# A hybrid decoder layer: cached-row attention started with each head's own column tiles, its products tied to the weight units, cached rows loaded some steps ahead

## The chip, the cores and the metric

The kernel runs on one core of a Trainium2 chip, as one launch. The metric is the device time of that launch in microseconds (us). TensorE (PE) multiplies matrices, VectorE (DVE), ScalarE (ACT) and GpSimd (POOL) do the elementwise work, and SyncE (SP) issues DMAs. Each engine works through its own instructions in order.

## The reference

One layer of a decoder for 512 prompt rows and 64 sample rows (8 sequences of 8 new tokens), model width 2048, all in float32:

```python
proj = rms_norm(x) @ w_in                       # 2048 -> 7168 columns, split among three mixers
ya = gate_b * causal_dwconv3(gate_c * xa)       # mixer A, 512 columns
for g, (window, dilation) in enumerate(((128, 1), (512, 4), (2048, 16))):
    # mixer B, 4 heads of 128: keys at distances 0, d, 2d, ..., window;
    # the sample rows read them from a cache of `window` K and V rows per sequence and head
    s_j = q . k[pos - j * d] / sqrt(128) - slope * j * d
    o_g, lse_g = softmax_j(s) @ v, logsumexp_j(s)
yb = sum_g softmax_g(lse) * o_g
yc = scale * ((trailing_mean_w(u) - u) @ w_pool)  # mixer C, w = 2, 4, 8, 16
x = x + concat(ya, yb, yc) @ w_out
x = x + (silu(dwconv3(h2 @ w_gate)) * (h2 @ w_up)) @ w_down     # h2 = rms_norm(x)
```

The outputs are the normed x and the new caches and states.

## The kernel before

Activations stand transposed: 128 features on the partitions, 576 tokens (512 prompt, 64 sample) along the free axis, as two halves of 288. A float32 product is made of three passes over rounded parts: weights are split into `wh` (ACT, L141) and `wl = wr - wh` (DVE, L142), activations likewise, and `mm3` (L150) adds wh·xh, wh·xl and wl·xh.

**Column tiles.** `project` (L159) makes one tile of 128 output columns from 16 blocks of w_in in two weight units of 8 blocks: one unit is a 512 KB load, one `wh`, one `wl` and 48 matmuls of 288 columns. Weight tiles have three buffers each, so `wl` of the next units is made while PE works on one. The accumulator `acc` has two buffers; a DVE instruction takes a finished tile out of PSUM, for attention into a tile `t` (L589, L592). Two of the tiles are made with the first norm, 54 more follow: 9 for each of 4 heads (q, k, v for three groups), 8 for pooling (4 each after the second and third head), 12 for the gated convolution. The out projection and the feed-forward part follow.

**What hangs on a head's tiles.** After each v tile, `natural` (L330) transposes that group's k and v on PE (L337, L346, L347) through the small PSUM tiles `ps` (two buffers), ACT copies them out, and DMAs store them into the outputs and into a DRAM scratch `kvd`. After the ninth tile `att_prompt` (L359) does the prompt attention on PE, DVE and ACT.

**Sample attention** is written as generators: `sample_scores` (L423) has 27 steps per head, one for 128x1024 products of the query broadcast `qb` with cached K rows `ek` (POOL, L433) and their row sums (DVE, L434); `sample_values` (L459) has 4 steps for the softmax, 13 for cached V rows `ev` (8 steps of eight DVE multiply-adds each for the far group, L516 and L519; 5 steps of `collect`, small matmuls, L497) and one for the new rows. `ek` has two buffers, `ev` three. After each column tile `step` (L562) lets the generators advance by the rates `RATE_MAIN`, `RATE_POOL`, `RATE_TAIL` (steps per tile, scores and values); a head's scores are queued after its ninth tile, its values after its scores. The scheduler then places the instructions of each engine; a load (`dma_paced`) is written in the step that uses it. All DMAs are issued by SP.

**Pooling tiles** (L622): `sp_nat` loads the old state, PE transposes it (L634), DVE copies it into `ec` (L636), POOL and DVE add shifted copies (L644), DVE forms `t` (L650, L652), ACT and DVE split it (L174, L175) into `ek` tiles, and `pool_map` (L666) multiplies two of those with a small weight, 24 matmuls on both `acc` buffers. `sp_nat` shares its two buffers (tag `ob`) with the output tiles of `att_prompt`.

Of the kernel before, what the change touches and what calls it, by code (L numbers as in the profile page):

```python
# [16 lines left out]
P = 128  # L17
# [23 lines left out]
RATE_MAIN = (2.5, 2.5)  # L41
RATE_POOL = (1.5, 1.0)
RATE_TAIL = (4.5, 5.0)
# [37 lines left out]
def decoder_step(ctx: ExitStack, tc, I, O):  # L81
    nc = tc.nc
    dma = nc.sync.dma_start
    PS = bass.MemoryType.PSUM
# [64 lines left out]

    def mm3(acc, wh, wl, xt, first, last):  # L150
        for h in range(2):
            xh = xt[:, 0, h * HALF:(h + 1) * HALF]
            xl = xt[:, 1, h * HALF:(h + 1) * HALF]
            o = acc[:, h, :HALF]
            nc.tensor.matmul(o, wh, xh, start=first, stop=False)  # L155
# [3 lines left out]
    def project(w, c0, xs, order, ahead=()):  # L159
        acc = acc_tile()  # L160
        n = len(order)
        for u in range(0, n, 8):
            ks = order[u:u + 8]
            k0 = min(ks)
            hi, lo = ahead[u // 8] if u // 8 < len(ahead) else wunit(w, k0, len(ks), c0)
            for j, k in enumerate(ks):
# [163 lines left out]
    def natural(g, h, k, v):  # L330

        for kv, t in ((0, k), (1, v)):
            blocks = [3] if g == 0 and kv == 0 else [0, 1, 2, 3]
            pt = ps_tile()
            for a in blocks:
                src = t[:, a * P:(a + 1) * P] if g == 0 else class_view(t, a)
                nc.tensor.transpose(pt[:, a * P:(a + 1) * P], src, ident)  # L337
            b0 = blocks[0]
            n = at.tile([P, 4, P], F32, tag=("kn", "vn")[kv], bufs=(1, 3)[kv], name=nm("nat"))
            nc.scalar.copy(n[:, b0:, :], pt[:, b0 * P:].rearrange("p (a d) -> p a d", d=P))  # L340
            if g == 0:
                dma(kvp[0][:, kv, h, :], n[:, 3, :])
            else:
                dma(kvp[g][:, kv, h, :].rearrange("(i r) d -> i r d", r=4), n)
        pt = ps_tile()
        nc.tensor.transpose(pt[:64, 0:P], smp(k), ident)  # L346
        nc.tensor.transpose(pt[:64, P:2 * P], smp(v), ident)  # L347
        ns = at.tile([64, 2 * P], F32, tag="ns", bufs=2, name=nm("ns"))
        nc.scalar.copy(ns, pt[:64, :2 * P])
        win = DILS[g][0]  # L350
        for kv in range(2):
            dma(kvs[g][:, win - 8:win, kv, h, :], ns[:, kv * P:(kv + 1) * P])
        dma(kvd[h].rearrange("(b i) v g d -> b i v g d", i=16)[:, 0:8, :, g, :], ns)
        return n
# [50 lines left out]
    def sample_queries(q):  # L405

        pt = ps_tile()
        for g in range(3):
            nc.tensor.transpose(pt[:64, g * P:(g + 1) * P], smp(q[g]), ident)
        qn = at.tile([64, 3 * P], F32, tag="qn", bufs=1, name=nm("qn"))  # L410
        nc.scalar.copy(qn, pt[:64, :3 * P])
        qd = dp.tile([3, 64, P], F32, name=nm("qd"))
        dma(qd.rearrange("g r d -> r g d"), qn.rearrange("r (g d) -> r g d", g=3))
        return qd
# [8 lines left out]
    def sample_scores(h, qd, st):  # L423

        for g in (2, 1, 0):
            qb = at.tile([P, 1024], F32, tag="qb", bufs=2, name=nm("qb"))
            dma_paced(qb, qd[g].rearrange("(b t) d -> b (t d)", b=NB).unsqueeze(1).to_broadcast([NB, 16, 1024]))
            qv = qb.rearrange("p (a j d) -> p j a d", a=2, d=P)
            rows = cache_rows(g, 0, h)

            def one(sl_, keys, prod):
                pv_ = prod.rearrange("p (a j d) -> p j a d", a=2, d=P)
                nc.gpsimd.tensor_mul(pv_, qv, keys)  # L433
                nc.vector.tensor_reduce(st[:, sl_, :].rearrange("p (j a) -> p j a", a=2), pv_, axis=AX.X, op=ALU.add)  # L434

            for u in range((1, 4, 8)[g]):
                kt = eslot_raw("ek", 1024)
                dma_paced(kt.rearrange("p (s d) -> p s d", d=P), rows[:, u])
                if g == 2:
                    one(19 + u, kt.rearrange("p (a j d) -> p j a d", j=4, d=P), kt)  # L440
                    yield
                    continue
                for e in range((8, 2)[g]):
                    nk = (1, 4)[g]
                    kb = kt[:, e * nk * P:(e + 1) * nk * P].rearrange("p (j d) -> p j d", d=P).unsqueeze(2)
                    one((e, 8 + 2 * u + e)[g], kb.to_broadcast([P, 4, 2, P]), prod_tile())
                    yield
            kn = at.tile([P, P], F32, tag="kvn", bufs=2, name=nm("kn"))
            dma_paced(kn, kvd[h][:, 0, g, :])
            one(16 + g, kn.unsqueeze(1).unsqueeze(1).to_broadcast([P, 4, 2, P]), prod_tile())  # L450
            yield
# [7 lines left out]
    def sample_values(h, st, yb):  # L459

        sx = st.rearrange("p s t -> p (s t)")
# [43 lines left out]
        for g in (2, 1, 0):  # L505
            rows = cache_rows(g, 1, h)
            for u in range((1, 4, 8)[g]):
                vt = eslot_raw("ev", 1024)
                v = vt.rearrange("p (s d) -> p s d", d=P)
                dma_paced(v, rows[:, u])  # L510
                if g == 2:
                    for t in range(8):
                        pos = 2 * (t % 4) + t // 4
                        w = st[:, 19 + u, pos:pos + 1]
                        if u:
                            nc.vector.scalar_tensor_tensor(av[:, t, :], v[:, t, :], w, av[:, t, :],  # L516
                                                           op0=ALU.mult, op1=ALU.add)
                        else:
                            nc.vector.tensor_scalar(av[:, t, :], v[:, t, :], w, None, op0=ALU.mult)  # L519
                elif g == 1:  # L520
                    collect([(j, ((8 + 2 * u + e) * 8 + 2 * j) * 8, v[:, 4 * e + j, :])
                             for e in range(2) for j in range(4)])
                else:
                    collect([(j, (i * 8 + 2 * j) * 8, v[:, i, :]) for i in range(8) for j in range(4)])
                yield
        vt = at.tile([P, 3, P], F32, tag="vnn", bufs=1, name=nm("vnn"))
        dma_paced(vt, kvd[h][:, 1])
        collect([(j, ((16 + g) * 8 + 2 * j) * 8, vt[:, g, :]) for g in range(3) for j in range(4)])
        yield
# [10 lines left out]
        if h == 3:  # L540
            late[7] = yb
        else:
            dma(y_d[4 + h], yb)


    scores, values = [], []
    clock = [0, 0.0, 0.0]
    hooks = {}
# [13 lines left out]
    def step(rs, rv):  # L562
        for fn in hooks.pop(clock[0], []):
            fn()
        clock[1] = pump(scores, clock[1] + rs)
        clock[2] = pump(values, clock[2] + rv)
        clock[0] += 1

    def in_proj(c0):
        return project(w_in, c0, xk, allk)  # L570
# [7 lines left out]
    def head_tiles(h):  # L578
        q, k, vn = [], [], []
        for g in range(3):  # L580
            for s in range(3):
                c0 = ATT0 + g * 1536 + s * 512 + h * P
                acc = None if c0 in first else in_proj(c0)
                t = t576()
                if c0 in first:
                    nc.vector.tensor_mul(t, first[c0], rstd1)
                    (q, k)[s].append(t)
                elif s == 0:
                    nc.vector.scalar_tensor_tensor(halves(t), acc, SC, halves(rstd1), op0=ALU.mult, op1=ALU.mult)  # L589
                    q.append(t)  # L590
                else:
                    nc.vector.tensor_mul(halves(t), acc, halves(rstd1))  # L592
                    if s == 1:
                        k.append(t)
                    else:
                        vn.append(natural(g, h, k[g], t))
                if (g, s) == (2, 2):
                    yb = at.tile([P, TOK], F32, tag="yb", bufs=2, name=nm("yb"))
                    att_prompt(h, q, k, vn, yb)
                    qd = sample_queries(q)  # L600
                    st = at.tile([P, 27, 8], F32, tag="st", bufs=2, name=nm("st"))
                    scores.append((sample_scores(h, qd, st),
                                   lambda: values.append((sample_values(h, st, yb), lambda: None))))
                yield
# [8 lines left out]
    def state_rows(src, n, outs):  # L613
# [5 lines left out]
        for dst, a, b in outs:  # L619
            dma(dst, so[a:b, :])  # L620
# [45 lines left out]
    def pool_map(gi, dsl):  # L666
        hi, lo = wload(pw[gi].rearrange("(k p) c -> p k c", p=P), 512, (("p (k c) -> p k c",), dict(k=2)))
        for m in range(2):
# [7 lines left out]
            dma(y_d[8 + j], z)  # L676
# [64 lines left out]
    def take(gen, n):  # L741
        for _ in range(n):
            if next(gen, gen) is gen:
# [690 lines left out]
```

## Time and profile before

| | us |
|---|---|
| median of three runs (2701.39 to 2705.43) | 2703.88 |
| the profiled execution | 2703.15 |
| its span | 2701.3 |
| PE busy in the span | 2563.4 (95%) |
| PE busy from 60 to 1050 us | 924.71 of 990 |
| DVE, ACT, POOL busy in the span | 1916.6, 959.8, 640.7 |

Matmuls are pipelined, so one that takes 300 ns follows the one before it after some 130 ns, and a busy PE is one that never ran dry. The column tiles and the attention lie in the stretch from 60 to 1050 us, with the first of the out projection.

### The profile page before, as it was taken

To read this page: it belongs to the slowest core of one execution; us is meant where nothing else is said; L and a number is where in the kernel's file an instruction comes from. 1 tells how busy PE (TensorE), PEld (TensorE's weight loads), DVE (VectorE), ACT (ScalarE), POOL (GpSimd) and SP (SyncE) were. 2 spreads that over 40 slices of the span, in tenths; PEclk is the share of its full clock that TensorE was granted. 3 is DMA by queue.
4 is the path that set the end of the run, shared out by engine and by line. 5 is a ranking of instruction groups with operands and counts; after the bars stand their busy time and mean duration, and the time that the engine had idled before them with its cause. 6 is when DMAs were issued, how large, how long until landed. Compare 5 with 4: busy or idle time off the path is not lost.

```text
span 2701.3 us, 48714 instructions
## 1 busy us (share of the span) xinstructions
PE 2563.4 (95%) x19855; PEld 2511.3 (93%) x19855; DVE 1916.6 (71%) x2664; ACT 959.8 (36%) x1393; POOL 640.7 (24%) x490
## 2 busy tenths in 40 slices
PE   8998998999898999999999999999999798989997
PEld 8988998998888899999999999999999797989897
DVE  5236468458567744488787888888887988898885
ACT  6121221221121233354444444444444434343335
POOL 0017126225436200012222221212121112121114
PEclk9998998999999999999999999999999899999999
DMA  8335258259547695645555555555555745545534
GB/s 259 112 99 158 79 165 233 76 151 242 141 124 201 189 285 187 195 140 169 163 169 156 175 156 168 164 166 170 168 164 169 261 139 162 158 145 150 166 91 144
DMA packets 605106, 446.31 MB, mean 165 GB/s; under 512 B 22423, under 2 KB 568898, under 8 KB 598482
## 3 DMA queue, kind: packets, MB, share of 16 engines
q1 hardware_dynamic: 604882, 443.19, 55.4%
q8 instruction: 156, 2.56, 0.4%
q14 instruction: 68, 0.56, 0.1%
HBM read 400.53 MB, written 129.86 MB: 196 GB/s over the span
## 4 chain that ended last, share of the span: by engine, by line
PE 72%; DVE 10%; DMA 7%; issue 5%; POOL 4%; ACT 1%; SPq 1%; DVEq 0%; POOLq 0%; ACTq 0%
PE acc L839 27%; PE pt L839 7%; PE ps L839 7%; PE acc L155 7%; PE s L839 7%; PE acc L156 7%; PE acc L157 7%; DMA ek<-in_cache_kv_w_dram 3%; DVE av L516 2%; POOL eq L433 2%; POOL prod L433 2%; DVE wl L142 1%; DVE wl L828 1%; DVE st L434 1%; DVE xs L175 1%
## 5 line engine op out<-in xcount | busy, mean ns | idle before, releaser
L155 PE MATMUL acc<-xs,wh 128*128 128x288 f32 x2208 | 664.6, 302 | 5.7 <-DVE t L700 3.9
L156 PE MATMUL acc<-xs,wh 128*128 128x288 f32 x2208 | 661.6, 300 | 0.0
L157 PE MATMUL acc<-xs,wl 128*128 128x288 f32 x2208 | 659.7, 299 | 0.7 <-DVE wl L142 0.7
L827 ACT ACTIVATE wh<-wr 128x640 fp32r<-128x640 f32 (+1 forms) x396 | 343.4, 876 | 642.7 <-DVE wr L889 189.6
L828 DVE TENSOR_TENSOR wl<-wr,wh 128x640 fp32r<-128x640 f32 (+1 forms) x396 | 416.6, 1059 | 104.6 <-ACT wh L827 100.7
L155 PEld LDWEIGHTS acc<-xs,wh 128*128 128x128 f32 x2208 | 421.2, 191 | 13.2 <-issue 8.8
L839 PE MATMUL acc<-xs,wh 128*128 128x288 f32 x2048 | 419.2, 296 | 9.6 <-DVE wk L1289 5.0
L157 PEld LDWEIGHTS acc<-xs,wl 128*128 128x128 f32 x2208 | 423.4, 192 | 3.2 <-issue 1.8
L156 PEld LDWEIGHTS acc<-xs,wh 128*128 128x128 f32 x2208 | 422.1, 191 | 2.9 <-issue 2.5
L141 ACT ACTIVATE wh<-wr 128x1024 fp32r<-128x1024 f32 (+1 forms) x150 | 155.6, 1038 | 568.8 <-PE acc L156 513.9
L839 PEld LDWEIGHTS acc<-xs,wh 128*128 128x128 f32 x2048 | 330.3, 189 | 12.1 <-DVE wk L1289 6.4
L142 DVE TENSOR_TENSOR wl<-wr,wh 128x1024 fp32r<-128x1024 f32 (+1 forms) x150 | 218.4, 1456 | 130.7 <-ACT wh L141 127.6
L839 PE MATMUL acc<-xs,wl 128*128 128x288 f32 x1024 | 302.1, 295 | 0.3 <-DVE wl L828 0.3
L839 PE MATMUL acc<-x,wh 128*128 128x288 f32 x1196 | 246.0, 297 | 8.1 <-ACT wh L827 8.1
L901 POOL TENSOR_TENSOR wx<-wx,wr 128x1024 f32<-128x1024 f32 x43 | 116.6, 2711 | 454.9 <-DVE wl L828 369.2
L839 PEld LDWEIGHTS acc<-x,wh 128*128 128x128 f32 x1196 | 193.7, 190 | 8.9 <-ACT wh L827 8.8
L828 DVE TENSOR_TENSOR wl<-wx,wh 128x1024 fp32r<-128x1024 f32 x129 | 168.7, 1308 | 46.0 <-ACT wh L827 44.4
L839 PEld LDWEIGHTS acc<-xs,wl 128*128 128x128 f32 x1024 | 193.3, 189 | 0.7 <-DVE wl L828 0.7
L839 PE MATMUL acc<-x,wl 128*128 128x288 f32 x598 | 178.2, 298 | 6.0 <-DVE wl L828 6.0
L827 ACT ACTIVATE wh<-wx 128x1024 fp32r<-128x1024 f32 x129 | 136.8, 1062 | 100.4 <-PE ps L839 37.5
L433 POOL TENSOR_TENSOR ek<-qb,ek 128x1024 f32<-128x1024 f32 x32 | 78.7, 2465 | 270.6 <-DMA qb<-qd 176.4
L839 PE MATMUL s<-xs,wh 128*128 128x288 f32 x660 | 138.7, 299 | 3.3 <-ACT wh L827 3.3
(402 smaller groups left out, 4988.8 us busy)
## 6 DMA issues: line engine op xcount, KB each, us to landing
out_dram<-in_cache_kv_w_dram SPq DMA_DIRECT2D x320, 204.0 KB
wr<-in_w_in_dram SPq DMA_DIRECT2D x110, 512.0 KB
wr<-in_w_down_dram SPq DMA_DIRECT2D x128, 320.0 KB
ek<-in_cache_kv_w_dram SPq DMA_DIRECT2D x52, 512.0 KB
ev<-in_cache_kv_w_dram SPq DMA_DIRECT2D x52, 512.0 KB
wx<-in_w_gate_dram SPq DMA_DIRECT2D x43, 512.0 KB
wr<-in_w_gate_dram SPq DMA_DIRECT2D x43, 512.0 KB
wr<-in_w_up_dram SPq DMA_DIRECT2D x43, 512.0 KB
```

The source lines that it names most:

```text
L141: nc.scalar.activation(hi[:, :n], dst, AF.Copy)
L142: low.tensor_sub(lo[:, :n], dst, hi[:, :n].bitcast(F32))
L155: nc.tensor.matmul(o, wh, xh, start=first, stop=False)
L156: nc.tensor.matmul(o, wh, xl, start=False, stop=False)
L157: nc.tensor.matmul(o, wl, xh, start=False, stop=last)
L175: nc.vector.tensor_sub(dst[1], src, dst[0].bitcast(F32))
L433: nc.gpsimd.tensor_mul(pv_, qv, keys)
L516: nc.vector.scalar_tensor_tensor(av[:, t, :], v[:, t, :], w, av[:, t, :], op0=ALU.mult, op1=ALU.add)
L827: nc.scalar.activation(hi[:, :n], src, AF.Copy)
L828: nc.vector.tensor_sub(lo[:, :n], src, hi[:, :n].bitcast(F32))
L839: nc.tensor.matmul(o, a[:, ws], b, start=first and k == 0 and i == 0, stop=k == n - 1 and i == 2, skip_group_check=True)
L901: nc.gpsimd.tensor_sub(b21, b21, b11)
```

## The change

The sample attention of a head is queued before its first tile, and each of its steps starts when what it needs is there (`have`). A head's tiles come in the order q0, k0, q1, k1, q2, k2, v0, v1, v2. The generators advance after each weight unit (`tick`, called in `project`) by half a rate, and the rates are new. Each product on POOL, and the first of the eight DVE instructions of a far V step, wait for the first matmul of the unit written last (`with_unit`). `in_turn` writes the loads of up to three steps ahead of the step that runs, as far as its buffers go. Far and near V steps alternate. The transposes of a tile (`rows_of`) and the prompt attention (`prompt`) are posted to a later tick. 113 output DMAs are issued by ACT (`adma`), in place of 93 by SP.

```diff
-RATE_MAIN = (2.5, 2.5)
-RATE_POOL = (1.5, 1.0)
-RATE_TAIL = (4.5, 5.0)
+RATE_MAIN = (2.3, 1.9)
+RATE_POOL = (2.0, 1.8)
+RATE_TAIL = (3.0, 3.2)
...
+    adma = nc.scalar.dma_start
...
+    def with_unit(ins):
+        tc.add_manual_dep(ins.ins, unit[0], mybir.DependencyInfo(mybir.DependencyClass.Sync,
+                                                                 mybir.DependencyReason.DATA),
+                          reason="paced by the products")
...
                 mm3(acc, hi[:, ws], lo[:, ws], xs[k], u + j == 0, u + j == n - 1)
+            unit[0] = mark[0].ins.name
+            if tick:
+                tick()
...
+        adma(kvd[h].rearrange("(b i) v g d -> b i v g d", i=16)[:, 0:8, kv, g, :], ns)
+        adma(kvs[g][:, win - 8:win, kv, h, :], ns)
...
+    def in_turn(steps, have, room):
+        at_ = [0]
+        def loads(to):
+            while at_[0] < min(to, len(steps)):
+                need, ls, _, keep = steps[at_[0]]
+                if not all(x in have for x in need) or (ls and keep >= 0 and sum(held_.values()) >= room):
+                    return
+                for load in ls:
+                    load()
+                if ls and keep >= 0:
+                    held_[keep] = 1
+                at_[0] += 1
+        held_ = {}
+        for i in range(len(steps)):
+            keep = steps[i][3]
+            while at_[0] <= i:
+                loads(i + 1)
+                if at_[0] <= i:
+                    yield
+            loads(i + 3)
+            steps[i][2]()
...
-                nc.gpsimd.tensor_mul(pv_, qv, keys)
+                with_unit(nc.gpsimd.tensor_mul(pv_, c["q"], keys))
...
+        yield from in_turn(group(0) + group(1) + group(2), have, 2)
...
+                if t == 0:
+                    with_unit(i_)
...
+        for i, n_ in enumerate(near):
+            steps.insert(2 * i + 1, n_)
+        steps.append(([("v", g) for g in range(3)], [load_new], new_sum, -1))
+        yield from in_turn(steps, have, 3)
...
-    def step(rs, rv):
+    def tick():
         for fn in hooks.pop(clock[0], []):
             fn()
-        clock[1] = pump(scores, clock[1] + rs)
-        clock[2] = pump(values, clock[2] + rv)
+        clock[1] = pump(scores, clock[1] + rate[0][0] / 2)
+        clock[2] = pump(values, clock[2] + rate[0][1] / 2)
         clock[0] += 1
...
+        for g, s in ((0, 0), (0, 1), (1, 0), (1, 1), (2, 0), (2, 1), (0, 2), (1, 2), (2, 2)):
...
+            post(1, lambda g=g, s=s, t=t: rows_of(g, s, t))
+            if (g, s) == (2, 2):
+                post(1, prompt)
+            yield
```

**The transposes after a v tile, on PE.** Before, second head, second group: `acc_300` is that v tile, `t576_307` holds it, and `acc_318` is the next tile.

```order
L157 MATMUL acc_300_2396<-xs_99_596,wl_306_2454 128x288
L337 MATMUL ps_308_2507<-ident_72,t576_296_2386 128x128 x4
L155 MATMUL acc_318_2542<-xs_24_151,wh_320_2545 128x288
...
L156 MATMUL acc_318_2542<-xs_56_318,wh_320_2545 128x288
L337 MATMUL ps_310_2515<-ident_72,t576_307_2505 128x128 x4
L346 MATMUL ps_312_2523<-ident_72,t576_296_2386 64x128
L347 MATMUL ps_312_2523<-ident_72,t576_307_2505 64x128
L157 MATMUL acc_318_2542<-xs_56_318,wl_321_2546 128x288
```

The transposes of `t576_307` stand 32 matmuls after the end of its tile. In the change that tile is `acc_385`, its copy `t576_405`, and `acc_406` is the tile after it:

```order
L168 MATMUL acc_385_2773<-xs_99_596,wl_394_2840 128x288
...
L168 MATMUL acc_406_2926<-xs_99_596,wl_416_3001 128x288
L351 MATMUL ps_417_3052<-ident_72,t576_405_2924 128x128 x4
L360 MATMUL ps_419_3060<-ident_72,t576_405_2924 64x128
L166 MATMUL acc_429_3092<-xs_24_151,wh_431_3095 128x288
```

They moved behind all 96 matmuls of the next tile.

**The same copy out of PSUM, on DVE.** Before, `L434` rows are sums of POOL's products, and `L592` is the copy:

```order
L142 TENSOR_TENSOR wl_324_2600<-wr_322_2597,wh_323_2599 128x1024
L434 TENSOR_REDUCE st_236_1765<-eq_328_2658 128x8
L434 TENSOR_REDUCE st_236_1765<-prod_338_2774 128x8
L434 TENSOR_REDUCE st_236_1765<-eq_341_2781 128x8
L592 TENSOR_TENSOR t576_307_2505<-acc_300_2396,rstd1_82 128x576
L142 TENSOR_TENSOR wl_332_2665<-wr_330_2662,wh_331_2664 128x1024
```

In the change (`L693` is the copy, `L490` the sums, `L584` far V steps):

```order
L584 SCALAR_TENSOR_TENSOR av_401_2909<-ev_404_2914,st_122_766,av_401_2909 128x128 x3
L693 TENSOR_TENSOR t576_405_2924<-acc_385_2773,rstd1_82 128x576
L584 SCALAR_TENSOR_TENSOR av_401_2909<-ev_404_2914,st_122_766,av_401_2909 128x128 x4
L143 TENSOR_TENSOR wl_432_3096<-wr_430_3093,wh_431_3095 128x1024
L490 TENSOR_REDUCE st_359_2614<-prod_411_2983 128x8
L562 COPY os_400_2908<-ps_413_2988 128x128
L584 SCALAR_TENSOR_TENSOR av_401_2909<-ev_404_2914,st_122_766,av_401_2909 128x128
L143 TENSOR_TENSOR wl_438_3165<-wr_436_3162,wh_437_3164 128x1024
```

Three sums in a row ahead of the copy became parts of one far V step, and the sums stand one by one between the units.

**The first pool map after the prompt attention, on PE.** Before, `ek_421` and `ek_441` are the split inputs of the first two pooling tiles, and `L634` the state transposes of the second and the fourth:

```order
L634 MATMUL ps_426_3286<-ident_72,sp_nat_425_3284 128x120
...
L155 MATMUL acc_467_3577<-ek_421_3273,wh_465_3573 128x288
...
L634 MATMUL ps_476_3621<-ident_72,sp_nat_475_3619 128x120
L155 MATMUL acc_467_3577<-ek_441_3418,wh_465_3573 128x288
```

In the change (`L729` are the state transposes of the second and third pooling tile, `L711` stores the new state, `ek_520` is the second tile's split input):

```order
L729 MATMUL ps_497_3472<-ident_72,sp_nat_496_3470 128x120
...
L711 MATMUL ps_508_3599<-ident_72,sst_491_3457 120x128
...
L166 MATMUL acc_539_3784<-ek_494_3465,wh_537_3780 128x288
...
L729 MATMUL ps_523_3646<-ident_72,sp_nat_522_3644 128x120
...
L166 MATMUL acc_539_3784<-ek_520_3639,wh_537_3780 128x288
L166 MATMUL acc_541_3800<-ek_520_3639,wh_537_3780 128x288
```

From the second tile's state transpose to the map that needs that tile there were 126 matmuls of 288 columns; now there are 44, because the transpose moved behind the prompt attention, whose output tiles hold the buffers of `sp_nat`.

## Rows read from the trace of the kernel before

**Rows 1.** The page's 40 equal slices of the span, some 67.5 us each.

```profile
PE   8998998999898999999999999999999798989997
...
DVE  5236468458567744488787888888887988898885
...
PEclk9998998999999999999999999999999899999999
```

**Rows 2.** Busy time by engine, TensorE clock, DMA share, 60 to 1050 us.

```profile
core 0: us, PE busy (x) PEld busy (x) DVE busy (x) ACT busy (x) POOL busy (x), PEclk, DMA share, GB/s
60.00:1050.00 990.00, 924.71 (x7740) 890.52 (x7739) 567.63 (x818) 217.19 (x307) 314.51 (x171) 0.96 0.58 162
```

**Rows 3.** Waits of PE, 60 to 1050 us: total us, times, longest.

```profile
PE ps L337 <- DVE t L592: 39.3, 6, 9.3
PE ps L497 <- DMA ev<-in_cache_kv_w_dram: 9.3, 4, 7.0
PE ps L468 <- DVE m L465: 6.4, 1, 6.4
PE acc L155 <- DVE t L700: 3.9, 1, 3.9
PE ps L482 <- DVE l L479: 1.7, 1, 1.7
```

**Rows 4.** Chain of waits, 240 to 258.3 us: start, us, what.

```profile
240.29 2.77 POOL prod L433
243.06 9.55 DMA ek<-in_cache_kv_w_dram
252.78 2.35 POOL eq L433
...
256.29 0.76 DVE t L592
257.09 1.13 PE ps L337 x4
```

**Rows 5.** Three windows after each other, columns as in rows 2.

```profile
247.80:257.10 9.30, 0.01 (x1) 0.01 (x1) 3.54 (x5) 0.00 (x0) 5.80 (x3) 0.67 0.63 136
257.10:262.00 4.90, 4.90 (x24) 4.83 (x25) 3.76 (x3) 0.97 (x3) 4.90 (x3) 0.58 0.45 119
262.00:270.00 8.00, 8.00 (x62) 8.00 (x61) 5.60 (x4) 2.00 (x2) 8.00 (x4) 1.00 0.37 109
```

**Rows 6.** DVE groups by line, 60 to 1050 us: busy us, mean ns.

```profile
L142 DVE TENSOR_TENSOR wl<-wr,wh 128x1024 fp32r<-128x1024 f32 (+1 forms) x127 | 192.4, 1515 | 106.3 <-ACT wh L141 103.3 <-DMA qd<-qn 2.8
L516 DVE SCALAR_TENSOR_TENSOR av<-ev,st,av 128x128 f32<-128x128 f32 x224 | 93.9, 482 | 0.0
L434 DVE TENSOR_REDUCE st<-eq 128x8 f32<-128x1024 f32 x38 | 46.1, 1214 | 45.1 <-POOL eq L433 45.1
...
L644 DVE TENSOR_TENSOR ec<-ec 128x708 f32<-128x708 f32 (+2 forms) x12 | 11.0, 920 | 7.0 <-POOL ec L644 6.8
...
L175 DVE TENSOR_TENSOR ek<-t,ek 128x576 fp32r<-128x576 f32 x8 | 6.9, 861 | 4.8 <-ACT ek L174 4.8
...
L650 DVE SCALAR_TENSOR_TENSOR t<-ec,ec 128x512 f32<-128x512 f32 x8 | 5.6, 694 | 0.1
...
L574 DVE TENSOR_TENSOR ec<-acc,rstd 128x288 f32<-128x288 f32 x8 | 3.6, 456 | 15.8 <-PE acc L157 15.8
```

**Rows 7.** POOL groups by line, same stretch and columns.

```profile
L433 POOL TENSOR_TENSOR prod<-qb,ek 128x1024 f32<-128x1024 f32 x32 | 85.0, 2658 | 18.8 <-DMA ek<-in_cache_kv_w_dram 11.8 <-DVE st L434 6.9
...
L644 POOL TENSOR_TENSOR ec<-ec 128x710 f32<-128x710 f32 x8 | 14.0, 1748 | 18.5 <-DVE ec L636 18.1 <-POOL npl L646 0.4
```

**Rows 8.** DVE groups by line, 60 to 150 us.

```profile
L142 DVE TENSOR_TENSOR wl<-wr,wh 128x1024 fp32r<-128x1024 f32 x14 | 17.2, 1226 | 36.8 <-ACT wh L141 36.8
```

**Rows 9.** DVE groups by line, 205 to 280 us.

```profile
L142 DVE TENSOR_TENSOR wl<-wr,wh 128x1024 fp32r<-128x1024 f32 x10 | 22.2, 2220 | 0.0
```

**Rows 10.** DMA issues of L352: ns min/median/max, first and last start us.

```profile
L352 SPq DMA_DIRECT2D out_dram<-ns x24: 622/644/1248, 69.4 to 736.7; - x24
```

More of the change, by code (lines that the diff above doesn't have):

```diff
@@ L154, in mm3, with project @@
             o = acc[:, h, :HALF]
-            nc.tensor.matmul(o, wh, xh, start=first, stop=False)
+            mark.append(nc.tensor.matmul(o, wh, xh, start=first, stop=False))
             nc.tensor.matmul(o, wh, xl, start=False, stop=False)
             nc.tensor.matmul(o, wl, xh, start=False, stop=last)
-    def project(w, c0, xs, order, ahead=()):
+    def project(w, c0, xs, order, ahead=(), tick=None):
         acc = acc_tile()
@@ L403, in att_prompt, with sample_query @@
                                   ot[:, :P].rearrange("p (r i) -> p r i", r=4))
-    def sample_queries(q):
+    def sample_query(q):
         pt = ps_tile()
[L408 to L413, printed above, removed]
+        nc.tensor.transpose(pt[:64, 0:P], smp(q), ident)
+        qn = at.tile([64, P], F32, tag="ns", bufs=3, name=nm("qn"))
+        nc.scalar.copy(qn, pt[:64, :P])
+        qd = dp.tile([64, P], F32, name=nm("qd"))
+        adma(qd, qn)
         return qd
@@ new lines, in new @@
+            def new():
+                one(16 + g, c["new"].unsqueeze(1).unsqueeze(1).to_broadcast([P, 4, 2, P]), prod_tile())
+            out = []
+            for u in range((1, 4, 8)[g]):
+                for e in range((8, 2, 1)[g]):
+                    loads = ([load_q] if u + e == 0 else []) + ([lambda u=u: load_k(u)] if e == 0 else [])
+                    out.append(([("q", g)], loads, lambda u=u, e=e: cached(u, e), 10 * g + u))
+            out.append(([("k", g)], [load_new], new, -1 - g))
@@ L526, in sample_values, with load_v, load_new @@
[L526 to L529, printed above, removed]
+        c = {}
+        def load_v(g, u):
+            vt = eslot_raw("ev", 1024)
+            c[g, u] = vt.rearrange("p (s d) -> p s d", d=P)
+            dma_paced(c[g, u], cache_rows(g, 1, h)[:, u])
+        def load_new():
+            c["new"] = at.tile([P, 3, P], F32, tag="vnn", bufs=1, name=nm("vnn"))
+            dma_paced(c["new"], kvd[h][:, 1])
@@ L579, in head_tiles @@
         q, k, vn = [], [], []
[L580 to L604, printed above, removed]
@@ new lines, in head_tiles, with rows_of, prompt @@
+        have, box = {}, {}
+        scores.append((sample_scores(h, have, box),
+                       lambda: values.append((sample_values(h, have, box), lambda: None))))
+        def rows_of(g, s, t):
+            if s == 0:
+                have["q", g] = sample_query(t)
+            elif s == 1:
+                natural(g, h, 0, t)
+                have["k", g] = True
+            else:
+                vn.append(natural(g, h, 1, t))
+                have["v", g] = True
+        def prompt():
+            yb = at.tile([P, TOK], F32, tag="yb", bufs=2, name=nm("yb"))
+            att_prompt(h, q, k, vn, yb)
+            have["y"] = yb
```

180 lines of the change are left out of this document (99 added, 81 removed).

## Prediction

> **What bounds the kernel now.** I read the page's slices first [rows 1]: PE is near full everywhere, and its dips of a tenth or two in the first 15 slices stand where its clock dips and where DVE is at 6 to 8 tenths. The windows by stage come next [rows 2]: in the 990 us from 60 to 1050 PE is busy 924.7, so it stands idle for 65.3 us, at a mean granted clock of 0.96, while DVE is busy for only 567.6 and POOL for 314.5. No other engine is full on average; PE waits for work that is late at certain places. PE's waits name these [rows 3]: five of them sum to 60.6 us, of which 39.3 are six waits of the transposes after a v tile for DVE's copy out of PSUM.
>
> Why the copy is late is read from the chain of waits of one of the six [rows 4]. POOL ended a product, waited 9.55 us until the next cached K rows were there, took 2.35 us for the next product, DVE summed it, and only then copied the tile in 0.76 us, because the sums stand ahead of the copy in its queue, as the order of DVE before shows. So a late cache load stops POOL, the sums stop DVE, and PE, whose next instruction wants the copy only 32 matmuls after the tile ended, stops for 9.3 us [rows 3].
>
> The wait costs more than its length. In the three windows after each other [rows 5] PE is empty for 9.3 us, then issues 24 instructions in 4.9 us at a mean clock of 0.58, so most of the time at the lower of its two levels (1.2 and 2.4 GHz), then 62 in 8.0 us at 1.00. At the last rate 24 take 3.1 us: the lower clock cost 1.8 us more. Nine waits of rows 3 are like that (six, and the longest of the next three lines): 9 x 1.8 = 16.2 us.
>
> **The change part by part.**
>
> *Transposes a tile later.* They now stand 96 matmuls behind the tile's end, at the 7.75 instructions per us of the full clock [rows 5] 12.4 us. The longest of the six waits came 32 matmuls and 9.3 us after the tile's end, 13.4 us in all; the mean one (39.3 / 6 = 6.6) some 11 us. So the old lateness is just covered, and the two consecutive sums ahead of the copy are gone too. I take all 39.3 as gained; the other end is one us left at each, 33.
>
> *Steps spread out, loads ahead.* The other 21.3 us of rows 3 (V rows that had not landed, the steps of the softmax, a copy at the start of the last column tiles) come from bursts of sample work at 2.5 and then 4.5 and 5 steps per tile; at two to three steps per tile, begun nine tiles earlier, each stands beside a tile's 12.4 us. I take all of it as gained; the other end is half, 10.7. Per unit of 48 matmuls (6.2 us) DVE has a `wl` of 1.5 us, half a copy of 0.8, 1.15 sums of 1.2 and 0.95 value steps, of which 8 in 18 are eight multiply-adds of 0.48 [rows 6]: 1.5 + 0.4 + 1.4 + 1.6 = 4.9 us, with the softmax and PSUM sums about 5.3. POOL has 1.15 products of 2.7 [rows 7]. Both fit, DVE not by much.
>
> *Products tied to the units.* POOL and the first far instruction now wait for a matmul. Behind them on DVE stand the `wl` of coming units and the copies. In the new order the `wl` of a unit stands about two units ahead of its use, and `acc` has a second buffer, so some 12 us of lateness pass unseen. I take nothing for this; without that cover it is the slower rival below.
>
> *Output DMAs on ACT.* One issue took 0.64 us on SP [rows 10]; 113 on ACT make 72 us beside 217 busy in 990 [rows 2]. ACT stays under a third, and its `wh` is as far ahead as `wl`. Nothing, then; if each of the 16 exponentials of the prompt attention stood behind three issues, 16 x 1.9 = 31 us would show.
>
> *Pool maps.* This is what I expect to cost. In the new order the second pooling tile's state transpose stands behind the prompt attention, and the map that needs the tile only 44 matmuls later; both `acc` buffers are then the map's, so nothing can go in between. After the second head PE needs 44 / 7.75 = 5.7 us and about 1 for small matmuls; the chain is a copy (0.3, like a small share of L574), POOL's add 1.75 [rows 7], three adds of 0.92, the difference 0.7 and its edge 0.4, the copy of the next tile 1.2 (L574 is 0.46 of it), a `wl` of 1.5 and four multiply-adds of 0.48, which stand between, and the split on ACT, 0.9 (as on DVE): 11.4 us [rows 6]. PE waits 11.4 - 6.7 = 4.7. Then the low part of the split, L175, stands behind seven more multiply-adds, an add and two more: 9 x 0.48 + 0.92 + 0.86 = 6.1, less 1 us of matmuls, another 5.1. After the third head there is one add, not three, 33 matmuls, and seven multiply-adds before the low part: 8.4 - 5.3 = 3.1 and 4.5 - 1 = 3.5. Together 16.4 us. Bounds: nothing if DVE runs these in the waits it has, 33 us if each of its instructions takes twice its time.
>
> *Prompt attention beside V steps.* In two of three prompt attentions a row maximum, on which the exponential and then PE wait, now stands behind seven multiply-adds (3.4 us) or five and a `wl` (3.9); part is covered by matmuls that stand between. I take 3 each, 6 us in all; bounds 0 and 8.
>
> *New low clock.* Three of these new waits are over 4 us: 3 x 1.8 = 5.4.
>
> The rest of the program has the same instructions, and I see nothing moved there. Sum, from the profiled execution's own time: 2703.15 - 60.6 - 16.2 + 16.4 + 6 + 5.4 = 2654. The median of the runs shown is 0.7 above that execution, so 2655 for a median.
>
> One row speaks against it. `wl` took 1.23 us while POOL was idle [rows 8] and 2.22 while POOL multiplied without pause [rows 9]. The Trainium skill (SBUF — State Buffer, Who interferes with whom) says why: a DVE instruction with two SBUF inputs and a POOL instruction that reads SBUF share one pair of ports, which the first holds for its whole length while the other stands still. The trace agrees, 2.22 against 1.23. By the row's mean over the stage, 1.5, which the sum uses, such waits are in the durations; by the rule at its hardest, a multiply-add or `wl` of every unit behind a product, the sum is that of the second rival.
>
> **Rivals.**
>
> *Nearly all waits go* (0.2). If DVE reaches the pool chains early, what is new shrinks to some 5 us: 2703.2 - 76.8 + 5 = 2631. For it: the average load of rows 2. Against it: the order, where 44 matmuls can't hold that chain.
>
> *DVE and POOL stand in each other's way* (0.13). With products in every unit, all 112 `wl` go at 2.22 [rows 9] in place of 1.5: 0.7 us more per unit on DVE, 5.3 + 0.7 = 6.0 of 6.2 us. That is the point where it decides: any unit with pooling or prompt attention on DVE is then over. In eight pooling and three attention tiles, 22 units, at 1.5 us over each: 33 us, 2655 + 33 = 2688. For it rows 9; against it that POOL is busy only half of a unit, and that its products don't run back to back any more.
>
> *Weights late, slower than before* (0.08). SP issues weight loads and row loads in one queue. A row load waits for a buffer that a tied product or multiply-add frees, and the weight loads behind it wait too. While that is under the two units of lead it shows nowhere; from there on each unit starts late by the whole excess. At 0.6 us in each of 108 units: 2655 + 65 = 2720. For it: rows 4, where rows took 9.55 us to come; against it that DMA is busy 0.58 of the stage [rows 2] and the same bytes are now spread evenly.
>
> *The change doesn't do what it says* (0.05). The scheduler may have issued loads as early as two K buffers allow already, and waits only change their place: 2700, give or take 4.
>
> **How the numbers follow.** The forecast, 2655 (its own range 2640 to 2672), has 0.54, the rivals the rest. The likeliest is 2655. The range goes down to the first rival with another 10 us, 2620, and up past the second to 2698, and leaves out the slower one and part of the last. About 0.2% (5.4 us) is what a measurement of this kernel can tell from no change. Faster by more: 0.54 + 0.2 + 0.13 and a little of the last, 0.87; slower 0.08; the same 0.05.
>
> **What would show it.** Right: PE's waits for the copy of a v tile gone; PE idle in 60 to 1050 us (now some 50 us shorter) about 28 us; the longest waits at the matmuls of the pool maps, for the split on ACT and DVE, in pairs after the second and the third head; a clock that dips there and nearly nowhere else; DVE's slices even. Wrong: PE waits for `wh` or `wl` in many tiles (weights late, or DVE full), `wl` over 2 us on average (ports), or waits of the transposes for ACT, whose DMA issues I took as hidden.

## The result, and the profile after

The changed kernel takes 2653.49 us (median of 4 runs, 2653.07 to 2655.56) against 2703.89 for the kernel before: a ratio of 0.9821, 95% interval 0.9808 to 0.9833. The profiled execution took 2653.72, with a span of 2651.9. So the time forecast, 2655, was met within 2 us. Whether the steps behind it were right is another question; the experiments answer it with no for the two largest terms, 39.3 and 21.3 us, and for the ties, which were priced at nothing.

The slices of the span after, to be laid beside [rows 1]:

```profile
PE   8999989999999999999999999999999798989997
...
DVE  5667866866866444688888887878787988898885
...
PEclk9999999999999999999999999999999799999999
```

In the first 15 slices the clock no longer dips and PE dips by a tenth only in the first and the sixth; DVE is at 4 to 8 tenths there, before at 2 to 8. The windows, columns as in [rows 2], first the whole stage (now 50 us shorter), then its parts (plain column tiles; the second prompt attention and the first pooling group; the same again; the last prompt attention and the tiles behind it):

```profile
60.00:1000.00 940.00, 914.19 (x7754) 881.21 (x7753) 627.76 (x818) 216.69 (x328) 311.15 (x171) 0.99 0.61 171
60.00:292.00 232.00, 232.00 (x1904) 226.06 (x1903) 154.20 (x143) 49.92 (x79) 93.06 (x37) 1.00 0.58 155
292.00:384.00 92.00, 81.17 (x776) 73.81 (x775) 68.60 (x127) 22.39 (x39) 32.04 (x24) 0.94 0.43 117
384.00:510.00 126.00, 125.78 (x1003) 123.59 (x1006) 91.96 (x97) 24.43 (x35) 51.92 (x21) 1.00 0.72 197
510.00:590.00 80.00, 74.87 (x737) 68.26 (x729) 58.82 (x107) 20.44 (x38) 30.87 (x24) 0.98 0.42 124
590.00:716.00 126.00, 126.00 (x1011) 123.82 (x1011) 89.70 (x94) 24.99 (x39) 53.72 (x23) 1.00 0.74 195
716.00:890.00 174.00, 165.10 (x1524) 156.85 (x1523) 116.74 (x196) 36.29 (x53) 49.53 (x43) 0.97 0.55 152
```

PE stands idle for 940 - 914.19 = 25.8 us, before 65.3 [rows 2]: 39.5 less. It is busy for 10.5 us less with 14 instructions more, since the clock is 0.99 in place of 0.96. Together that is 50.0 us, and the whole span lost 49.4. The plain column tiles, where the six waits for v copies of [rows 3] stood, have 0.2 us of idle time left in 484; all that remains is at the prompt attentions, the pooling tiles and the end of the sample work. PE's waits in the same stage (total, times, longest):

```profile
PE s L379 <- DVE sb L390: 5.6, 1, 5.6
PE pt L401 <- ACT sb L396: 2.8, 2, 2.4
PE ps L729 <- DMA sp_nat<-in_state_pool_dram: 2.8, 1, 2.8
PE s L379 <- DVE t L751: 2.3, 1, 2.3
PE ps L559 <- ACT so L713: 2.2, 1, 2.2
PE ps L612 <- DVE os L564: 1.7, 2, 1.4
PE ps L711 <- DVE os L564: 1.4, 1, 1.4
PE ps L729 <- DVE os L564: 1.3, 1, 1.3
...
PE acc L166 <- ACT t L770: 1.0, 2, 0.8
PE ps L729 <- ACT so L713: 0.9, 1, 0.9
PE acc L166 <- ACT ek L189: 0.9, 2, 0.7
...
PE acc L167 <- DVE ek L190: 0.3, 1, 0.3
```

The copies of the v tiles are gone from the list. L379 and L401 belong to the prompt attention, 10.7 us; L729, L711, L713, L559 and `ek` to the pooling tiles, 11.2 with a 0.4 us wait that is not shown; the rest, 3.9, to the sample work and one `wl`. DVE's groups show what else changed; they answer to [rows 6]:

```profile
L143 DVE TENSOR_TENSOR wl<-wr,wh 128x1024 fp32r<-128x1024 f32 (+1 forms) x127 | 219.3, 1728 | 76.6 <-ACT wh L142 76.2 <-DMA wr<-in_w_in_dram 0.2
L584 DVE SCALAR_TENSOR_TENSOR av<-ev,st,av 128x128 f32<-128x128 f32 x224 | 109.8, 546 | 51.0 <-DMA ev<-in_cache_kv_w_dram 46.6 <-PE acc L166 4.2
L490 DVE TENSOR_REDUCE st<-prod 128x8 f32<-128x1024 f32 x54 | 65.3, 1210 | 36.9 <-POOL prod L489 36.9
L490 DVE TENSOR_REDUCE st<-eq 128x8 f32<-128x1024 f32 x54 | 65.3, 1210 | 22.7 <-POOL eq L489 22.7
```

DVE waits for POOL's products for 36.9 + 22.7 = 59.6 us in front of its sums; before, it was 45.1 for `eq` [rows 6], 37.6 for `ek` and 32.6 for `prod`, together 115.3. But a `wl` now takes 1.73 us on average and a far multiply-add 0.55, where it was 1.52 and 0.48: DVE is busy 60 us longer with the same number of instructions, 818.

### The profile page after: what moved, and what is told of

The parts are those of the page before. It is cut to its first block, busy times and chain, and to the rows that moved or that the text cites. A ratio compares the mean times of both kernels' runs of the same rounds, so it can differ in the third digit from the quotient of the medians.

```text
span 2651.9 us, 48799 instructions
## 1 busy us (share of the span) xinstructions
PE 2551.9 (96%) x19855; PEld 2500.7 (94%) x19855; DVE 1976.2 (75%) x2664; ACT 958.8 (36%) x1413; POOL 637.1 (24%) x490
## 4 chain that ended last, share of the span: by engine, by line
PE 57%; DVE 6%; DMA 3%; issue 1%; ACT 1%; SPq 0%; POOL 0%; DVEq 0%; ACTq 0%; POOLq 0%
PE acc L927 28%; PE ps L927 7%; PE pt L927 7%; PE s L927 7%; PE acc L166 2%; PE acc L168 2%; PE acc L167 2%; DVE wl L916 1%; DVE xs L190 1%; DMA ev<-in_cache_kv_w_dram 1%; DMA al<-act 1%; DMA wr<-yd 1%; DVE av L584 0%; DVE wk L1377 0%; PE acc L1485 0%
## 5 line engine op out<-in xcount | busy, mean ns | idle before, releaser
L927 PE MATMUL acc<-xs,wh 128*128 128x288 f32 x2048 | 417.6, 295 | 10.8 <-DVE wk L1377 5.8
L143 DVE TENSOR_TENSOR wl<-wr,wh 128x1024 fp32r<-128x1024 f32 (+1 forms) x150 | 245.3, 1636 | 102.1 <-ACT wh L142 101.8
L489 POOL TENSOR_TENSOR eq<-qb,ek 128x1024 f32<-128x1024 f32 x48 | 122.8, 2557 | 223.2 <-PE acc L166 106.8
L489 POOL TENSOR_TENSOR prod<-qb,ek 128x1024 f32<-128x1024 f32 x48 | 119.1, 2480 | 184.0 <-PE acc L166 124.3
```

Of the source, the lines that this page charges most:

```text
L143: low.tensor_sub(lo[:, :n], dst, hi[:, :n].bitcast(F32))
L489: with_unit(nc.gpsimd.tensor_mul(pv_, c["q"], keys))
L927: nc.tensor.matmul(o, a[:, ws], b, start=first and k == 0 and i == 0, stop=k == n - 1 and i == 2, skip_group_check=True)
```

## The experiments

The theory that stood in the prediction: the later transposes cover the late copies (39.3 us and six low clocks), spreading and early loads remove the other waits, and the ties carry nothing. Its rivals put the gain into the ties, or into the spread steps alone. Ratios are to the kernel before, timed on the same chip; one thousandth is 2.7 us.

**The parts undone one by one.** Without ties (`with_unit` gone from both places):

```
-                with_unit(nc.gpsimd.tensor_mul(pv_, c["q"], keys))
+                nc.gpsimd.tensor_mul(pv_, c["q"], keys)
...
-                if t == 0:
-                    with_unit(i_)
```

> The changed kernel without with_unit: products and far sums wait for their data alone. By the prediction (the ties were priced at nothing): 2653.5, give or take 5, and PE waits nowhere for the copy of a v tile. Rival, the ties keep DVE free: POOL's products bunch up, wl goes above its mean of 1.74 us, and waits of PE for wl or for a copy come back: 2665 or more. Second rival, the ties cost time, as POOL waits 231 us in 60:1000 for a matmul: under 2645.

Measured: ratio 0.9988 (0.9976 to 1.0001). The gain is gone, within what these runs can tell, though transposes, rates and loads were all as in the change: my step for the ties, nothing, was wrong by (0.9988 - 0.9821) x 2703.9 = 45 us. The rows show how. DVE's groups, 60 to 1030 us, of the kernel without ties:

```profile
L143 DVE TENSOR_TENSOR wl<-wr,wh 128x1024 fp32r<-128x1024 f32 (+1 forms) x125 | 178.3, 1427 | 64.7 <-ACT wh L142 62.2 <-DMA out_dram<-in_cache_kv_w_dram 2.1 <-DMA wx<-in_w_gate_dram 0.2
...
L490 DVE TENSOR_REDUCE st<-eq 128x8 f32<-128x1024 f32 x54 | 65.6, 1215 | 87.2 <-POOL eq L489 87.2
L490 DVE TENSOR_REDUCE st<-prod 128x8 f32<-128x1024 f32 x54 | 65.6, 1214 | 75.0 <-POOL prod L489 75.0
```

DVE stood 162.2 us in front of sums whose product was not there, 59.6 with ties. Its `wl` was faster, 1.43 us, so the rival's "wl goes above 1.74" failed; it is waiting, not slowness. One such place in the timeline (start, duration, what; in brackets the idle time before it and who ended it):

```profile
465.47 2.34 POOL L489 TENSOR_TENSOR eq<-qb,kn 128x1024 f32<-128x1024 f32 x1 [9.72 <-DMA kn<-kvd]
...
467.85 1.22 DVE L490 TENSOR_REDUCE st<-eq 128x8 f32<-128x1024 f32 x1 [8.09 <-POOL eq L489]
...
469.28 0.21 DVE L534 COPY mb<-m 8x128 f32<-8x128 f32 x1
469.43 1.20 DVE L143 TENSOR_TENSOR wl<-wr,wh 128x1024 fp32r<-128x1024 f32 x1
...
469.64 0.20 PE L537 MATMUL ps<-ident,mb 8*128 8x8 f32 x1 [4.63 <-DVE mb L534]
```

The chain is that of [rows 4]: a row comes late (here a new K row, read back from `kvd`), POOL waits 9.72 us, the sum 8.09, and a 0.21 us copy queued behind the sum makes PE wait 4.63. Only the victim is another: `mb`, not the copy of a v tile, which is now read a tile later. PE's waits in this kernel are 14.8 us for `mb`, 12.4 for `os`, 8.0 for `sb`.

Transposes back behind their own tile's copy:

```
-            post(1, lambda g=g, s=s, t=t: rows_of(g, s, t))
+            rows_of(g, s, t)
```

> The changed kernel with the transposes of a tile written right behind its copy, so about 27 matmuls (3.5 us) behind the tile's end in place of 96; all else as changed. By the prediction, which gives the whole 39.3 us and six low clocks to the later transposes: 2653.5 + 39.3 + 10.8 = 2704. Rival, the spread steps and early loads have made the copies early by themselves: the ten copies that ended 3.9 to 7.5 us after their tile in the changed kernel would hold PE by 14 us in all, hardly one for 4 us: 2668 to 2671.

Measured: 0.9853 (0.9832 to 0.9873), 8.7 us more than the change by the ratios (the two intervals just touch), nowhere near 50. The waits for copies came back small, as the rival had it:

```profile
PE ps L351 <- DVE t L693: 10.9, 7, 3.7
```

Loads written at their own step (`loads(i + 3)` dropped; `loads(i + 1)` remains):

> The changed kernel with each cached row loaded when its own step is written, not two steps ahead. By the prediction (loads ahead share the 21.3 us, and POOL's wait for K rows is what stopped DVE): POOL waits 5 to 10 us for K rows in many steps, the near sums on PE wait for V rows, some 2 us each in 24 steps: 2690 to 2720. Rival, the scheduler issues a load as soon as its buffer is free wherever it is written, and two to three buffers set how far ahead it is: 2653.5, give or take 5.

Measured: 0.983 (0.9813 to 0.9846), not told apart from the change. The loads ahead carry nothing that these runs can see.

The old steps per tile:

```
-RATE_MAIN = (2.3, 1.9)
-RATE_POOL = (2.0, 1.8)
-RATE_TAIL = (3.0, 3.2)
+RATE_MAIN = (2.5, 2.5)
+RATE_POOL = (1.5, 1.0)
+RATE_TAIL = (4.5, 5.0)
```

> The changed kernel with the steps per tile of the kernel before (2.5 and 2.5, 1.5 and 1.0, 4.5 and 5.0). By the prediction, which gives 21.3 us and three low clocks to steps spread out and loads ahead: 2665 to 2680, with waits for the softmax and for V rows back in the last column tiles. Rival, the ties hold any two steps apart whatever the rate, and the early loads did nothing measurable either: 2653.5, give or take 5.

Measured: 0.9845 (0.9821 to 0.9869), some 6 us; the intervals overlap. The waits for V rows did not return, and for the softmax one of 2.9 us did. In this kernel, where each step keeps its tie to a unit, the numbers of the rates carry little.

The output DMAs back on SP (`adma = nc.sync.dma_start`):

> The changed kernel with the 113 output DMAs issued by SP again. By the prediction, which priced the move to ACT at nothing: 2653.5, give or take 5. Rival, on SP they stand ahead of weight and row loads, wait there for ACT's copies and hold the loads up: 2665 or more, with PE or DVE waiting for wr, ek or ev. Second rival, ACT does better without them: under 2647.

Measured: 0.9819 (0.9804 to 0.9834), the same. Nothing, as forecast.

**One part done alone.** The kernel before with the transposes of the first two v tiles of a head a tile later:

```
-                    else:
-                        vn.append(natural(g, h, k[g], t))
+                    elif g < 2:
+                        post(1, lambda g=g, t=t: vn.append(natural(g, h, k[g], t)))
+                    else:
+                        vn.append(natural(g, h, k[g], t))
```

> The kernel before with one edit: the transposes of the k and v tiles of the first two groups posted a tile later, nothing else. By the prediction: 39.3 us and six low clocks of 1.8 gone, 2703.9 - 50 = 2654, with the waits for V rows and the softmax (21 us) still there. Rival, the lateness of DVE then shows at wl or at other instructions behind the sums, and the gain needs the spread steps: 2680 or more.

Measured: 0.9978 (0.9965 to 0.9991): 6 us, where the prediction's own step gives 50. PE is idle for 60.8 us in the stage, before for 65.3. Its waits, 60 to 1050 us, beside [rows 3]:

```profile
PE acc L157 <- DVE wl L142: 16.6, 12, 3.6
PE ps L497 <- DVE os L502: 15.2, 2, 11.3
PE ps L497 <- DMA ev<-in_cache_kv_w_dram: 14.6, 7, 6.7
PE ps L468 <- DVE m L465: 5.7, 1, 5.7
```

The 39.3 us for the copies are gone and 16.6 for `wl`, 15.2 for `os` and 5.3 more for `ev` have come. DVE waits for POOL's products for 111.5 us (39.2 for `eq`, 43.0 for `ek`, 29.3 for `prod`), before for 115.3, so it is as late as it was, and PE meets it at the next thing in its queue.

The kernel before with ties alone (to the two units of the tile just written, in turn, since its steps are made once a tile):

```
+    def with_unit(ins):
+        ties[0] += 1
+        tc.add_manual_dep(ins.ins, units[-1 - ties[0] % 2], ...
...
-                nc.gpsimd.tensor_mul(pv_, qv, keys)
+                with_unit(nc.gpsimd.tensor_mul(pv_, qv, keys))
...
+                        if t == 0:
+                            with_unit(i_)
```

> The kernel before with one addition: every product and the first far multiply-add of a step tied, as in the change, to the first matmul of one of the two units of the column tile just written, in turn. The steps of a tile and the places of the transposes and loads stay. In DVE's order 56 of the 108 sums now stand alone behind a wl of their own, 40 before. Theory, bunched sums are what made the copies late, and a tie alone parts some of them: 2675 to 2692, with the waits for the v copies about half of 39.3 us. Rival, ties help only together with spread steps and loads ahead: 2698 to 2704.

Measured: 0.9968 (0.9957 to 0.9978), 9 us, a little short of the range of the theory; the v copies still cost 25.9 us:

```profile
PE ps L349 <- DVE t L606: 25.9, 5, 7.3
```

In the trace 45 of the 108 sums stand alone behind a `wl`, before 25 (the expectation says 56 and 40). So neither part alone gives more than 9 of the 48 us. The later transposes aren't what the ties lack, since the change without them still gains 40 us (0.9853); it is among the steps per unit, the early start and the other parts of the change.

**What of the tie works.** The tie is two things: an edge that the scheduler sees when it orders the queues, and a semaphore wait on the chip. The first can be had without the second:

```
-        ... mybir.DependencyInfo(mybir.DependencyClass.Sync, ...
+        ... mybir.DependencyInfo(mybir.DependencyClass.NoSync, ...
```

> The changed kernel, the tie kept as an order for the scheduler but without a semaphore wait on the chip. In DVE's order the sums of the products then stand about one to a unit's wl as in the changed kernel (numbers of wl ahead of the first sums: 12 12 13 13 13 14 15 15 16 17 18 19), where without ties they bunch (12 12 13 13 13 14 14 14 15 15 16 16). Theory, the order carries the 45 us that the kernel without ties lost: 2653.5, give or take 6, and DVE waits for POOL some 60 us as in the changed kernel (162 without ties). Rival, the wait on the chip carries it by holding POOL off DVE: 2680 or more.

Measured: 0.9807 (0.9786 to 0.9827), as good as the change at least. The 261.5 us for which POOL waits for PE in the changed kernel are gone, and DVE's waits for POOL are 20.3 + 16.0 = 36.3 us:

```profile
L490 DVE TENSOR_REDUCE st<-prod 128x8 f32<-128x1024 f32 x54 | 65.4, 1210 | 20.3 <-POOL prod L489 20.3
L490 DVE TENSOR_REDUCE st<-eq 128x8 f32<-128x1024 f32 x54 | 65.2, 1207 | 16.0 <-POOL eq L489 16.0
```

The order carries the gain; the wait on the chip carries none of it. DVE is busy for 580.9 us from 60 to 1000 us, 46.9 less than in the changed kernel, yet PE's idle time is the same, 25.1 against 25.8. What the order is shows in the number of `wl` that stand ahead of each of the first 20 sums in DVE's queue:

```
changed kernel    12 12 13 13 14 15 15 16 17 18 19 20 21 22 22 23 24 25 26 27
tie, order only   12 12 13 13 13 14 15 15 16 17 18 19 20 21 22 22 23 25 25 26
no ties           12 12 13 13 13 14 14 14 15 15 16 16 16 17 17 18 18 19 20 21
```

Of the 108 sums 74 stand alone behind a `wl` in the changed kernel, so one to a unit of 48 matmuls, and the rest in pairs; with the order only 57 stand alone and three once together; without ties 20 stand alone, and three or four together eleven times. DVE then reaches sums whose rows have not come: apart from its very first wait of some 60 us, POOL waits 244.7 us for cached K rows without ties, 87.2 with the order only and 78.7 in the change. The edge also shifts the cached row loads among the weight loads in SP's queue, so DVE's order as the one that matters is read from these waits; no run changes it alone.

Ties on the products alone, the far multiply-adds free:

> The changed kernel with the tie on POOL's products alone; the first far multiply-add of a step waits for its data only. Theory, bunched sums that wait for POOL are what stopped DVE: 2653.5, give or take 6. Rival, the far sums (some 4 us of DVE each) put early ahead of copies and wl are as bad as the sums: 2675 or more.

Measured: 0.987 (0.9849 to 0.9891), 13 us more than the change, between the two: the far multiply-adds need their edge too, but the larger part of the 45 us is the products'. DVE waits for POOL for 63.3 us here and 59.6 in the change, and 74 sums stand alone in both, so these 13 us are not lost in front of the sums; PE's longest waits are for `sb` (13.0) and `os` (7.4). That is the kind of loss that the rival named, at less than its 2675.

**Towards a better version.** Two edits against what is left: the four row blocks of a prompt attention in four units, and buffers of their own for `sp_nat` and `so`.

```
-                post(1, prompt)
+                for T in range(4):
+                    post(1 + T, lambda T=T: prompt(T))
...
-                sp_nat = at.tile([120, P], F32, tag="ob", bufs=2, name=nm("sp_nat"))
+                sp_nat = at.tile([120, P], F32, tag="spn", bufs=2, name=nm("sp_nat"))
-        so = at.tile([n, P], F32, tag="so", bufs=1, name=nm("so"))
+        so = at.tile([n, P], F32, tag="so", bufs=2, name=nm("so"))
```

> The changed kernel with the four row blocks of a prompt attention in four successive units in place of one, and with own buffers for the pool state rows (two for so, two for sp_nat apart from ob). In 60:1000 us of the changed kernel PE stands idle 25.8 us, of which 10.8 are at the score and transpose matmuls of the prompt attention and 6.6 at so and sp_nat. Theory, these 17 us and two or three low clocks of 1.8 go: 2632 to 2640. Rival, DVE is what is late there, and the waits move to the next matmul that needs it: 2648 to 2656.

Measured: 0.9786 (0.9766 to 0.9806), 2644.3 us, between the two expectations. The buffers alone:

> The changed kernel with own buffers for sp_nat and two for so, the prompt attention as in the change. Theory, of the 9 us that the version with both edits gained, the buffers account for the 6 us of waits for so and sp_nat: 2646 to 2650, with PE's longest wait still the 5.6 us one in front of the last prompt attention. Rival, these waits only uncover DVE being late for the pool chain: 2652 to 2656.

Measured: 0.9817 (0.9794 to 0.9839): nothing. Its waits for `sp_nat` and `so` are gone and others for DVE's `ec` and `os` have come. So the 9 us point to the prompt attention in four units, by itself or with the buffers; it was not run alone, and the intervals of the two versions overlap. Both edits with the tie as an order only:

> The version with both edits (prompt attention in four units, own buffers), its ties an order only, without a wait on the chip. Theory, the wait on the chip makes POOL's products start with a unit, where wl runs on DVE (wl's mean is 1.67 us with it, 1.56 without), so DVE gains some 45 us of its own time and reaches the late places sooner: 2637 to 2642. Rival, DVE is late there by its order, not by its speed: 2642 to 2647.

Measured: 0.9738 (0.9723 to 0.9754), 2629.09 us, below the range of the theory and by the ratios 22 us faster than the changed kernel. Its stage, columns as in [rows 2], PE's longest waits, and `wl`:

```profile
60.00:1000.00 940.00, 931.96 (x7916) 899.60 (x7915) 568.53 (x831) 224.59 (x337) 335.48 (x171) 0.99 0.63 175
```

```profile
PE s L379 <- DVE sb L390: 3.1, 1, 3.1
PE ps L612 <- DVE os L564: 1.6, 1, 1.6
```

```profile
L143 DVE TENSOR_TENSOR wl<-wr,wh 128x1024 fp32r<-128x1024 f32 (+1 forms) x131 | 182.3, 1391 | 87.9 <-ACT wh L142 79.8 <-DMA x1d<-wk 5.2 <-DMA out_dram<-in_cache_kv_w_dram 2.1
```

PE's idle time in 940 us is 8.0, and DVE is busy for 59 us less than in the changed kernel, with 13 instructions more.

## Why the prediction came out right, step by step

**The diagnosis held.** A late row stops POOL, the sum stops DVE, and something short behind the sum stops PE. DVE waits for POOL for 115.3 us before, 111.5 with the later transposes alone (0.9978), 101.3 with the ties alone (0.9968) and 162.2 without ties (0.9988), but for 59.6 in the change (0.9821) and 36.3 with the order only (0.9807). The waits tell the slow kernels from the fast ones; they are no price, as 162.2 and 115.3 give the same time, and 63.3 goes with 0.987.

**"Transposes a tile later ... I take all 39.3 as gained" failed.** The arithmetic on that wait was right (done alone, the waits for the copies vanish), but it priced the victim, not the cause. DVE was as late as ever, and 6 of 50 us came. The step lacked the sentence on what is late next. With DVE in time, the later transposes are worth 8.7 us.

**"I take nothing" for the ties failed** by 45 us. I read them as a wait on the chip, looked for what they could delay, and did not look for what they do to DVE's order, though the order was there to be read: mostly one sum to a `wl`, where the kernel before has up to four together.

**Spread steps and loads ahead, 21.3 us:** the waits went, as forecast, but not for that reason. Old rates cost 6 us, late loads nothing measurable. What the change seems to need of the spreading is a step per unit, so that a tie has a unit to go to; the ties on the kernel before, with steps per tile, gave 9 us. That is an inference from this pair: ticks per unit, the early start and the new order of the tiles were neither undone nor run alone. Nor was a part that the description of the change leaves out: before, POOL writes a far product over the K rows in `ek`, whose buffer then waits for DVE's sum, and SP's row loads (L129) wait 46.8 us for sums; in the change the product has a tile of its own, and these waits are gone. It doesn't make the gain without the ties (0.9988), but whether the ties need it is open.

**Output DMAs, nothing:** right.

**Pool maps, 16.4 us:** 11.2, at other matmuls. The maps' own waits are 2.2 (1.2 for the split `ek`, 1.0 for `t`, which frees their `acc`); 9.0 stand ahead of them, at the state transposes and sums, where PE was held for a row load, for `so` and for `os`. While it stood there the chain that I had costed ran on. Own buffers for two of these moved the waits and gained nothing, which points at DVE's lateness there and not at the buffers. So the sign "the longest waits at the matmuls of the pool maps" did not come. In the working, the terms listed give 9.6 and 4.2 us after the third head (two adds, 1.8 us, fewer), not 8.4 and 4.5; that moves the sum by less than 1 us.

**Prompt attention, 6 us:** 10.7. The longest wait, 5.6 us, is not the row maximum that I named but the score's own evacuation `sb`. DVE ahead of it, in the timeline:

```profile
725.65 1.21 DVE L490 TENSOR_REDUCE st<-prod 128x8 f32<-128x1024 f32 x1
726.78 3.23 DVE L584 SCALAR_TENSOR_TENSOR av<-ev,st,av 128x128 f32<-128x128 f32 x4
729.93 0.74 DVE L795 TENSOR_TENSOR t<-acc,rstd 128x576 f32<-128x576 f32 x1
730.60 1.21 DVE L143 TENSOR_TENSOR wl<-wr,wh 128x1024 fp32r<-128x1024 f32 x1
...
731.93 0.41 DVE L390 SCALAR_TENSOR_TENSOR sb<-cst,s 128x256 f32<-128x256 f32 x1
```

A sum, four multiply-adds, a copy and a `wl` stand in front of a 0.41 us instruction. Here the multiply-adds took 0.81 us each, not the 0.48 of [rows 6], beside a product on POOL (727.00 to 729.34), which had waited 3.26 us for its tie.

**Clock:** forecast -16.2 + 5.4 = -10.8, measured as PE's busy time, -10.5, with 14 instructions more in it (1.8 us at 7.75 per us). Three waits over 4 us were forecast and one came, but the clock also fell to 0.63 behind the 2.8 us wait for `sp_nat`.

**The sum** was -60.6 + 16.4 + 6 for idle time, -38.2; the trace has -39.5. It is right because the waits of [rows 3] did go, whatever took them away, and the rest is luck: two errors in the new waits (5.2 too much, 4.7 too little) cancel, and 3.9 at sample work that were not forecast are made up for by 4.7 of smaller waits before (65.3 - 60.6) that were not counted and went too. Had the change come without its ties, the same working would have said 2655 for a kernel that takes some 2700.

**Rivals:** that DVE and POOL stand in each other's way came true in the durations (`wl` 1.52 to 1.73 us), but cost PE nothing that the runs can tell in the changed kernel: with the order only DVE is busy for 46.9 us less and PE's idle time stays. (In [rows 9] POOL did not multiply "without pause": it is busy for 54.4 of the 75 us, so the 2.22 is a mean with gaps in it.) Late weights did not show (0.7 us for `wl`, none for `wh`).

## What to carry to other kernels

When an engine is late, ask first why it is late, and price a change that only moves the reader of its results at little: the next instruction in that queue inherits the wait. Read an added dependency as an edit of the order, engine by engine, before you read it as a wait; and try it as an order only, since the order gave the whole gain here and the wait none. Work that is off the path but shares a queue with work on it did least harm here when it was laid one piece to a unit of the main work.

## What the runs showed of the hardware

A `wl` (two SBUF inputs on DVE) and a product on POOL that overlap do not share time; the one that starts later waits for the other. In the trace of the changed kernel the 40 `wl` of 128x1024 that start inside a product take 2.75 us on average, the 271 that meet none 1.23. There, with the tie's wait on the chip, a product starts with its unit and `wl` 0.78 us after it:

```profile
138.65 2.40 POOL L489 TENSOR_TENSOR prod<-qb,ek 128x1024 f32<-128x1024 f32 x1 [4.00 <-PE acc L166]
139.43 2.70 DVE L143 TENSOR_TENSOR wl<-wr,wh 128x1024 fp32r<-128x1024 f32 x1 [2.57 <-ACT wh L142]
```

`wl` ends at 142.13, 1.08 us after the product's end at 141.05: it took 2.70, not the 1.23 of [rows 8], and the product is not slowed. In the last version, both edits with the tie as an order only, it is often the other way about; 29 products start inside a `wl` there and take 3.24 us on average:

```profile
132.23 1.22 DVE L143 TENSOR_TENSOR wl<-wr,wh 128x1024 fp32r<-128x1024 f32 x1
132.39 3.33 POOL L489 TENSOR_TENSOR eq<-qb,ek 128x1024 f32<-128x1024 f32 x1 [7.68 <-DVE st L490]
```

`wl` takes 1.22 us and the product 3.33 in place of 2.40. This is what the Trainium skill says (SBUF — State Buffer, Who interferes with whom), that the order of issue decides which of the two blocks; the trace agrees, 2.70 and 3.33. Of 1.5 us lost by DVE or 0.9 by POOL the second is the smaller, and in neither trace does PE wait for POOL directly from 60 to 1000 us. That this alone made the 13 us between the last two versions with both edits is not shown: the order of the queues differs between them too.
